# Hybrid decoder layer on one core: right-hand tiles moved by 32 bytes, value compression by broadcast behind the first value matmuls, decay series moved

## The chip, the cores and the metric

One core of one Trainium2 chip runs the whole layer in one launch. The metric is the device time of one execution in microseconds, taken over several runs; the median is compared. Engines are named as in the profile: PE is the matrix engine (PEld its weight loads), DVE the vector engine, ACT the activation engine, POOL the general engine, SP the engine that issues most DMAs.

## What is computed

The layer takes `x` of 512 tokens by 1024 and returns the same shape. All is float32.

```
h = rms_norm(x, norm1_g); proj = h @ w_in          # split into rx, rgate, q, kc, vc, ks, vs, kw, vw, gates
y_rnn = (rg_lru(causal_dwconv(rx)) * gelu(rgate)) @ w_rnn_out
   # rg_lru: log_a = 8 * r * log_sigmoid(lru_lambda); h_t = a_t h_{t-1} + u_t
v_cmp = gelu(blocks(vc) @ cmp_w1_v) @ cmp_w2_v     # 31 compressed positions, 4 groups, 64 wide; k_cmp alike, then normed
o = gates * (softmax(q k_cmp) v_cmp, softmax(q k_slc) v_slc, softmax(q k_win) v_win)    # 16 heads, 4 groups
x = x + (sigmoid(mg_rnn) * y_rnn + sigmoid(mg_attn) * (o @ w_attn_out)) @ w_out
x = x + (gelu(gate) * val) @ w_down                # gate, val = causal_dwconv(rms_norm(x) @ w_up)
```

## The kernel before

Activations stand with channels on the 128 partitions and the 512 tokens along the row. Each weight arrives as a tile of 128 x 1024 from one packed array `in_w`, in the order of a plan. `_wprep` (L115 to 138) issues its DMA on SP into one of two `wraw` tiles, ACT rounds it into `whi` (L124), and DVE, or POOL during the heads, subtracts to get the low half `wlo` (L131, or L129 in pieces of 256 columns). Three buffers each of `whi` and `wlo` stand between that and PE. A product of float32 accuracy is three matmuls (`mm3`, L153 to 155): high weight by high activation, high by low, low by high. Here the activation is the moving operand (512 columns) and the weight the loaded one; in the value projections (L669 to 671, L701 to 703) it is the other way about.

The stages, by their time in the profile: the first norm with the projections for the compressed keys and values (to 43 us); `before_heads` (to 88 us), with keys of the first pair, the hidden layers of the two compressors (`compress_hid`), two query projections, `compress_out` and `v_pair0`; sixteen heads with the other projections filled in between (to 383 us); the output projection of attention, `attn_out`, which reads `oh` and `ol` (383 to 428 us); the recurrent part (to 565 us); `merge`, whose matmuls read `hgh` and `hgl` (565 to 628 us); `w_out`, which reads `mh` and `ml` (to 671 us); the feed-forward part, whose last stage reads `fh` and `fl`.

PE's order is the order of the code (`manual_schedule`). On the other engines a scheduler sets the order of the instructions from its own estimate; `high_priority` moves one ahead in it, and `issue_after` keeps one behind a named instruction. `later` and `tick` hold small PE steps back by a number of yields of the running generator.

Tiles come from pools at either end of the memory. Pools with `side="right"` grow down from its upper end: `ea1`, `ea2` (L256, L258), `otp` with `ot`, `otl` with `oh` and `ol`, and `hgp` with `hgh`, `hgl`, `iv` and `g`. In the built program these start 32 bytes past a multiple of 64 (`oh` at 180192, `ol` at 196576, `hgh` at 186336). The tiles of the left side, with `xh`, `xl`, `mh`, `ml`, `fh`, `fl` (this one from 155840 to 204992) and the three buffers of each weight half, start at multiples of 64.

`compress_hid("v")` ends with the gelu `hidv` (L517) and then makes the four copies of it that fill 128 columns: four casts on ACT into `hv` (L524) and four subtractions on DVE into `hvl` (L525). `compress_out` (L528 on) multiplies these, as loaded weights, by the second layer (L537 to 539), then the keys' `hk` by theirs (L153 to 155 with 128 columns). After it `v_pair0` (L661 on) runs eight steps `k` with twelve matmuls of 304 columns each, from three weight tiles of three steps.

`lru_c8` (L890 on) works out `8 * log_sigmoid(lru_lambda)` by a series of 25 DVE instructions on 128 x 11 values (L896 to 907). It is called in `attn_out` after the fourth of eight output columns (L871); its result is first read in the recurrent part. The scheduler put the 25 into DVE's order in the first head.

Of the kernel before, what the change touches and what calls it, by code (L numbers as in the profile page):

```python
# [8 lines left out]
F32 = mybir.dt.float32  # L9
# [38 lines left out]
MS_L, KL1, KL2, QN_L = 3, 12, 14, 6  # L48

MS1, RT1, SQ_W = 2, 7, 4  # L50
HPRI = 200

EARLY = "mmSSSmmSSmSm"

RNN_STEPS = ("rx0 rx1 rx2 rx3 rg0 rx4 rx5 rg1 scan0 rgate0 rgate1 rg2 rgate2 rgate3 rx6 gelu0 rx7 rgate4 rgate5 rg3 "
             "scan1 rx8 rx9 rgate6 rx10 rgate7 gelu1 rgate8 rg4 rg5 scan2 rgate9 gelu2")
# [46 lines left out]
class Kern:  # L103
# [123 lines left out]
    def build(self):  # L227
        tc, nc, a = self.tc, self.nc, self.a
        tp = lambda name, **kw: tc.tile_pool(name=name, bufs=1, reuse_waits="tile", **kw)
        L = ExitStack()  # L230
        with L:
            self.cst = L.enter_context(tp("cst"))
            self.wp = L.enter_context(tp("wp"))
            xp = L.enter_context(tp("xp"))
            drp = L.enter_context(tc.tile_pool(name="drp", bufs=1, space=bass.MemoryType.DRAM))
            self.mg = {}
            for n in ("mga", "mgr"):
                for c in range(8):
                    self.mg[n, c] = drp.tile([128, S], F32, name=f"{n}{c}")
            self.pp = self.cst.tile([128, NP_], F32, name="pp")  # L240
            self.cc = self.cst.tile([128, NC_], F32, name="cc")
            self.ones = self.cst.tile([128, 128], F32R, name="ones")
            self.rstd = self.cst.tile([128, S], F32, name="rstd")
            self.rstdt = self.cst.tile([128, 4], F32, name="rstdt")
            nc.scalar.dma_start(self.pp, a["pp"])
            self.ident = self.cc[:, C_ID:C_ID + 128]
            self.xh = xp.tile([128, KO, S], F32R, name="xh")
            self.xl = xp.tile([128, KO, S], F32R, name="xl")

            R2 = ExitStack()  # L250
            with R2:
                with tp("at") as self.at, ExitStack() as at_ps, tc.manual_schedule(engines={mybir.EngineType.PE}):
                    self.ps = at_ps.enter_context(tp("psA", space=PSUM))
                    self.mmb = 2
                    self.early = 0
                    with tp("ea1", side="right") as self.ea:  # L256
                        pss = self.norm1()
                    with tp("ea2", side="right") as self.ea:  # L258
                        self.before_heads(pss)
                    self.early = None  # L260
                    otp = R2.enter_context(tp("otp", side="right"))
                    self.ot = otp.tile([128, KO, S], F32, name="ot")
                    self.mgo = at_ps.enter_context(tp("mgo"))
                    self.pool_lo = True
                    with tp("hd") as self.hd:
                        fills = self.heads()
                    otl = R2.enter_context(tp("otl", side="right"))
                    self.out_split(otl)
                    for _ in fills:
                        self.tick()  # L270
                    self.pool_lo = False
                mgp = L.enter_context(tp("mgp"))
                self.ma = mgp.tile([128, KO, S], F32, name="ma")
                PB = ExitStack()
                self.ps = PB.enter_context(tp("psB", space=PSUM))
                self.mmb = 7
                self.attn_out()
            with tp("hgp", side="right") as self.hgp:
                self.hgh, self.hgl = {}, {}
                self.wpri = 80  # L280
                with tp("rnn") as self.rn:
                    self.rnn()
                self.wpri = 0
                with tp("mrg") as self.mr:
                    self.mh = self.mr.tile([128, KO, S], F32R, name="mh")
                    self.ml = self.mr.tile([128, KO, S], F32R, name="ml")
                    self.merge()
                    self.xn = mgp.tile([128, KO, S], F32, name="xn", tag="ma")
                    self.w_out()
            with tp("ff") as self.ff:  # L290
                self.ffn()
            PB.close()
# [11 lines left out]
    def norm1(self):  # L304
# [50 lines left out]
        def token_rstd():  # L355
# [6 lines left out]
            w = at.tile([128, 4], F32, name="rsw")  # L362
            with self.tc.high_priority(HPRI):
                nc.vector.tensor_scalar(m, ms[:, :, 0], 1.0 / D, EPS, op0=ALU.mult, op1=ALU.add)
# [4 lines left out]
        def row_rstd():  # L369

            pt = self.ps.tile([128, S], F32, name="T", bufs=2)
            for t in range(4):
                nc.tensor.transpose(pt[:, 128 * t:128 * t + 128], e[:, t], self.ident)
            with self.tc.high_priority(HPRI):
                nc.scalar.copy(self.rstd, pt)
# [7 lines left out]
    def before_heads(self, pss):  # L383
        nc, at = self.nc, self.at

        self.gkq = self.cst.tile([128, 3], F32, name="gkq")
        nc.vector.tensor_scalar(self.gkq, self.pp[:, P_KS:P_KS + 3], self.pp[:, P_QG:P_QG + 1], None, op0=ALU.mult)

        self.G = at.tile([128, 4, 48], F32, name="G")
        self.kfull, self.kraw, self.qs, self.rq, self.V, self.qms = {}, {}, {}, {}, {}, {}  # L390

        self.compress_in("k", pss[:2])
        self.compress_in("v", pss[2:])
        self.run(self.k_pair(0))
        self.pool_lo = True
        self.run(self.compress_hid("k"))
        self.run(self.q_proj(0))
        self.later(1, lambda: self.k_fin(0))
        self.later(1, lambda: self.k_fin(1))
        self.run(self.compress_hid("v"))  # L400
        self.run(self.q_proj(1))
        self.later(4, lambda: self.q_norm(0))
        self.run(self.compress_out())
        self.run(self.v_pair0())

    def later(self, n, f):

# [87 lines left out]
    def compress_hid(self, kind):  # L495
        nc, at = self.nc, self.ea
        ch = getattr(self, "ch" + kind)
        ps = self.mmps()[:, 0:272].rearrange("p (s g i) -> p s g i", s=2, g=4)
        for m in range(16):
            if m % 8 == 0:  # L500
                wh, wl = self.w("w1" + kind, m // 8)
            col = slice(128 * (m % 8), 128 * (m % 8) + 128)
            q = m // 8
            nc.tensor.matmul(ps.rearrange("p s g i -> p (s g) i"), wh[:, col],
                             ch[:, :, :, m % 8, q:q + 34].rearrange("p s g i -> p (s g) i"),
                             start=(m == 0), stop=False)
            nc.tensor.matmul(ps[:, 0], wl[:, col], ch[:, 0, :, m % 8, q:q + 34],
                             start=False, stop=(m == 15))
            if m % 3 == 2:
                yield  # L510
        t = at.tile([128, 4, 34], F32, name="ct", bufs=2)
        nc.scalar.copy(t, ps[:, 1])
        nc.vector.tensor_add(t, t, ps[:, 0])
        b = at.tile([128, 1], F32, name="cb", bufs=2)
        nc.vector.tensor_copy(b, t[:, 0, 32:33])
        hid = at.tile([128, 4, 32], F32, name="hid" + kind)
        nc.scalar.activation(hid, t[:, :, 0:32], AF.Gelu_apprx_tanh, bias=b)  # L517
        if kind == "k":
            self.hk = at.tile([128, 2, 128], F32R, name="hk")
            self.split(self.hk[:, 0], self.hk[:, 1], hid.rearrange("p g i -> p (g i)"))  # L520
        else:
            self.hv = [at.tile([128, 4, 4, 32], F32R, name=n) for n in ("hv", "hvl")]
            for r in range(4):
                nc.scalar.copy(self.hv[0][:, :, r], hid)  # L524
                nc.vector.tensor_sub(self.hv[1][:, :, r], hid, self.hv[0][:, :, r].bitcast(F32))  # L525

    def compress_out(self):
        nc, at, keep = self.nc, self.ea, self.at  # L528
# [222 lines left out]
    def cmp_probs(self, g):  # L751
# [7 lines left out]
        pl = self.hd.tile([128, S], F32R, name="cpl", bufs=1)  # L759
        with self.tc.high_priority(HPRI):  # L760
            self.split(ph, pl, T)
# [96 lines left out]
    def attn_out(self):  # L858
        nc, oh, ol = self.nc, self.oh, self.ol
        self.last_tab = self.last_exp  # L860
        for k in range(KO):
            nc.sync.dma_start(self.ma[:, k], self.mg["mga", k])
            self.tab(self.ma[:, k], self.ma[:, k], AF.Sigmoid)
        for m in range(8):
            wt = self.w("ao", m)
            ps = self.ps.tile([128, S], F32, name="mm", bufs=self.mmb)
            for k in range(KO):
                self.mm3(ps, wt, slice(128 * k, 128 * k + 128), (oh[:, k], ol[:, k]), k == 0, k == KO - 1)
            nc.vector.tensor_mul(self.ma[:, m], ps, self.ma[:, m])
            if m == 3:  # L870
                self.c8 = self.lru_c8()  # L871

    def tab(self, *args, **kw):

# [365 lines left out]
```

## Time and profile before

| | |
|---|---|
| median of 3 runs | 1068.7 us (1066.21 to 1070.89) |
| the profiled execution | 1069.39 us, span of its instructions 1067.6 us |
| PE busy, of the span | 98% (1048.5 us) |
| DVE, ACT, POOL busy | 67%, 53%, 18% |
| DMA queues, memory rate | 96 GB/s mean |
| PE's waits | 1.84 us and 1.29 us between 67 and 70.5 us, 1.93 us at 115 us |

The rows further on come from this one execution. Starts are microseconds from the start of the span. A matmul's duration in a row is longer than its share of PE's time, since the next one begins before it ends: PE's pace is read from the starts. PEclk is the clock granted to PE as a share of 2.4 GHz.

### The profile page before, as it was taken

Reading aid. Unit: us, or ns where it says so; the run is one execution under the profiler, and the core shown is the slowest. Engines: PE = TensorE matmul, PEld = TensorE weight load, DVE = VectorE, ACT = ScalarE, POOL = GpSimd, SP = SyncE. Lnnn points to the kernel's source line nnn. Section 1 sums busy time; section 2 is a strip of 40 time slices with the busy share of each in tenths; the row PEclk is TensorE's granted clock in tenths of the full one; section 3 lists DMA queues with packets and bytes.
Section 4 is the critical chain, followed back from the end, with each engine's and each line's share of the span. In section 5 each row is a group of like instructions: output and inputs, shape, how many; then the busy total and the mean of one; then the engine's idle time right before and its main releaser. Section 6 shows DMA issues by size and latency. Waiting matters only on the chain.

```text
span 1067.6 us, 13868 instructions
## 1 busy us (share of the span) xinstructions
PE 1048.5 (98%) x5023; PEld 875.7 (82%) x5023; DVE 714.2 (67%) x1359; ACT 565.2 (53%) x953; POOL 192.6 (18%) x324
## 2 busy tenths in 40 slices
PE   9989999999999999999999999999999999999998
PEld 7888788978888888887877888888888888888886
DVE  6767879877777643789698564777777777732221
ACT  6366677878767641477667433444444444421110
POOL 0356325135252210231312003100000000000000
PEclk9999899999999999999999999999999999999999
DMA  6421211011221262443333534232223332333330
GB/s 242 96 98 60 59 60 40 21 70 50 67 73 67 94 195 92 116 145 103 119 100 107 197 109 148 89 109 92 97 91 95 99 99 99 99 109 119 109 112 26
DMA packets 44452, 106.04 MB, mean 99 GB/s; under 512 B 13231, under 2 KB 14639, under 8 KB 44384
## 3 DMA queue, kind: packets, MB, share of 16 engines
q1 hardware_dynamic: 41632, 102.26, 29.7%
q0 software_dynamic: 2608, 2.76, 1.1%
q8 instruction: 39, 0.64, 0.2%
q14 instruction: 29, 0.24, 0.1%
q10 hardware_dynamic: 144, 0.15, 0.0%
HBM read 96.10 MB, written 6.29 MB: 96 GB/s over the span
## 4 chain that ended last, share of the span: by engine, by line
PE 76%; DVE 11%; ACT 8%; issue 2%; DMA 2%; POOL 1%; SPq 0%; DVEq 0%; ACTq 0%
PE mm L153 22%; PE mm L155 22%; PE mm L154 22%; PE O L815 3%; ACT s L797 2%; PE T L824 2%; DMA wraw<-in_w 2%; ACT whi L124 1%; PE S L786 1%; DVE wlo L131 1%; PE S L787 1%; DVE s L790 1%; DVE ptl L179 1%; DVE iv L977 1%; ACT pth L178 1%
## 5 line engine op out<-in xcount | busy, mean ns | idle before, releaser
L124 ACT CAST whi<-wraw 128x1024 fp32r<-128x1024 f32 (+2 forms) x167 | 172.6, 1034 | 231.9 <-PE mm L154 199.5
L153 PE MATMUL mm<-xh,whi 128*128 128x512 f32 x744 | 292.6, 393 | 0.5 <-ACT hgh L178 0.5
L155 PE MATMUL mm<-xh,wlo 128*128 128x512 f32 x744 | 291.4, 392 | 1.0 <-DVE wlo L131 1.0
L154 PE MATMUL mm<-xl,whi 128*128 128x512 f32 x744 | 291.0, 391 | 0.0
L131 DVE TENSOR_TENSOR wlo<-wraw,whi 128x1024 fp32r<-128x1024 f32 (+1 forms) x131 | 158.5, 1210 | 93.2 <-ACT whi L124 91.9
L155 PEld LDWEIGHTS mm<-xh,wlo 128*128 128x128 f32 x744 | 140.2, 188 | 31.3 <-DVE wlo L131 1.4
L153 PEld LDWEIGHTS mm<-xh,whi 128*128 128x128 f32 x744 | 140.3, 189 | 29.2 <-ACT hgh L178 0.9
L154 PEld LDWEIGHTS mm<-xl,whi 128*128 128x128 f32 x744 | 140.3, 189 | 28.5
L129 POOL TENSOR_TENSOR wlo<-wraw,whi 128x256 fp32r<-128x256 f32 (+1 forms) x140 | 101.5, 756 | 221.9 <-ACT whi L124 188.3
L797 ACT ACTIVATE s<-s,bs,rq 128x128 f32<-128x128 f32 (+3 forms) x128 | 82.5, 648 | 19.4 <-DVE bs L794 19.3
L153 PE MATMUL mm<-fh,whi 128*128 128x512 f32 x192 | 74.7, 389 | 0.0
L154 PE MATMUL mm<-fl,whi 128*128 128x512 f32 x192 | 74.7, 389 | 0.0
L155 PE MATMUL mm<-fh,wlo 128*128 128x512 f32 x192 | 74.7, 389 | 0.0
L1080 DVE SCALAR_TENSOR_TENSOR y<-u,pp,y 128x512 f32<-128x512 f32 x96 | 71.7, 749 | 2.0 <-ACT y L1078 0.4
L179 DVE TENSOR_TENSOR ptl<-T,pth 128x512 fp32r<-128x512 f32 x80 | 55.0, 687 | 21.1 <-ACT pth L178 20.7
L790 DVE CUSTOM_DVE_ANT_0 s<-S,cc 128x128 f32<-128x128 f32 (+3 forms) x128 | 58.0, 483 | 6.9 <-PE S L787 6.5
L178 ACT CAST pth<-T 128x512 fp32r<-128x512 f32 x80 | 46.5, 581 | 28.4 <-PE T L824 27.9
L1076 DVE TENSOR_TENSOR u<-mm,rstd 128x512 f32<-128x512 f32 x48 | 33.0, 688 | 40.8 <-PE mm L155 40.8
L824 PE MATMUL T<-cc,s 128*128 128x128 f32 x320 | 48.8, 274 | 1.3 <-DVE ptl L179 0.8
L824 PEld LDWEIGHTS T<-cc,s 128*128 128x128 f32 x320 | 39.5, 141 | 12.5 <-DVE ptl L179 1.3
L1075 POOL MEMSET u<- 128x2 f32 x48 | 4.7, 100 | 246.0 <-DVE y L1080 241.7
L178 ACT CAST fh<-y 128x512 fp32r<-128x512 f32 x24 | 14.9, 621 | 63.7 <-DVE y L1087 63.7
(299 smaller groups left out, 1870.1 us busy)
## 6 DMA issues: line engine op xcount, KB each, us to landing
wraw<-in_w SPq DMA_DIRECT2D x158, 512.0 KB, 3.4
x<-in_x SPq DMA_DIRECT2D x8, 256.0 KB, 4.5
mga<-mgo SPq DMA_DIRECT2D x8, 256.0 KB, 2.0
mgr<-mgo SPq DMA_DIRECT2D x8, 256.0 KB, 2.5
ma<-mga SPq DMA_DIRECT2D x8, 256.0 KB, 4.3
sg<-mgr SPq DMA_DIRECT2D x8, 256.0 KB, 3.6
xr<-in_x SPq DMA_DIRECT2D x8, 256.0 KB, 2.7
out<-y SPq DMA_DIRECT2D x8, 256.0 KB, 2.0
```

The source lines that it names most:

```text
L124: self.last_hi = nc.scalar.copy(hi[:, :n], raw[:, :n])
L129: nc.gpsimd.tensor_sub(lo[:, e], raw[:, e], hi[:, e].bitcast(F32))
L131: nc.vector.tensor_sub(lo[:, :n], raw[:, :n], hi[:, :n].bitcast(F32))
L153: nc.tensor.matmul(ps, wh, xh, start=first, stop=False)
L154: nc.tensor.matmul(ps, wh, xl, start=False, stop=False)
L155: nc.tensor.matmul(ps, wl, xh, start=False, stop=last)
L178: self.nc.scalar.copy(hi, src)
L179: self.nc.vector.tensor_sub(lo, src, hi.bitcast(F32))
L790: nc.vector.tensor_tensor_reduce(s[i, x], ps[:, x - xs[0]], mask, 1.0, -3e38, ALU.add, ALU.max, mx[:, x, i:i + 1])
L797: self.last_exp = nc.scalar.activation(s[t, x], s[t, x], AF.Exp, bias=bs[:, x, t:t + 1], scale=rq[:, t], accum_out=sm[:, x, t:t + 1])
L824: nc.tensor.transpose(T[:, off:off + 128], s[i, x][:, 128 * j:128 * j + 128], self.ident)
L1080: nc.vector.scalar_tensor_tensor(y, u[:, j:j + S], pc(P_FW, j * nu + c), y, ALU.mult, ALU.add)
```

## The change

The right-hand side gets a first tile of 32 bytes, so that every right-hand tile moves down by 32 bytes (`oh` to 180160, `ol` to 196544, `hgh` to 186304) and starts at a multiple of 64. The four casts and four subtractions for `hv` and `hvl` become one of each, reading `hidv` by broadcast, and get the priority. The first four yields of `v_pair0` (two of its eight steps, 24 matmuls) run before `compress_out`; for that the accumulator of the values' second layer moves from the tag `S` to `mm`. The 25 instructions of the decay series are kept behind the fourth `ma` product.

```diff
-EARLY = "mmSSSmmSSmSm"
+EARLY = "mmSSSmmSSmmm"
+VP0 = 4
...
+            L.enter_context(tp("rpad", side="right")).tile([128, 8], F32, name="rpad")
...
+        v = self.v_pair0()
+        for _ in range(VP0):
+            next(v)
+            self.tick()
         self.run(self.compress_out())
-        self.run(self.v_pair0())
+        self.run(v)
...
-            for r in range(4):
-                nc.scalar.copy(self.hv[0][:, :, r], hid)
-                nc.vector.tensor_sub(self.hv[1][:, :, r], hid, self.hv[0][:, :, r].bitcast(F32))
+            h4 = hid.rearrange("p g (o i) -> p g o i", o=1).to_broadcast([128, 4, 4, 32])
+            with self.tc.high_priority(HPRI):
+                nc.scalar.copy(self.hv[0], h4)
+                nc.vector.tensor_sub(self.hv[1], h4, self.hv[0].bitcast(F32))
...
-            nc.vector.tensor_mul(self.ma[:, m], ps, self.ma[:, m])
+            ins = nc.vector.tensor_mul(self.ma[:, m], ps, self.ma[:, m]).ins
             if m == 3:
-                self.c8 = self.lru_c8()
+                with self.tc.issue_after(ins):
+                    self.c8 = self.lru_c8()
```

The new lines shift the numbers: a line of the changed program stands up to ten lower (L537 becomes L546, L669 becomes L678).

PE, at the end of the second query projection, before (`em` the accumulator, `hv` and `hvl` the value copies):

```order
L155 MATMUL em<-xh,wlo 128x512
L537 MATMUL em<-whi,hv 128x64
L538 MATMUL em<-wlo,hv 128x64
L539 MATMUL em<-whi,hvl 128x64
L537 MATMUL em<-whi,hv 128x64
```

and the same place in the changed program (`v_724` to `v_727` are the accumulators of `v_pair0` for its four blocks of 128 tokens):

```order
L156 MATMUL em<-xh,wlo 128x512
L678 MATMUL v_724<-whi,xh 128x304
L679 MATMUL v_724<-wlo,xh 128x304
L680 MATMUL v_724<-whi,xl 128x304
L678 MATMUL v_725<-whi,xh 128x304
...
L679 MATMUL v_727<-wlo,xh 128x304
L680 MATMUL v_727<-whi,xl 128x304
L546 MATMUL em<-whi,hv 128x64
```

The matmuls on `hv` stood right behind the projection; 24 value matmuls, with four small `hsq` matmuls among them, now stand between.

DVE in the first head, before, between the score maxima of head 1 (`ISA s,mx`) and the copy of `qms` that frees an accumulator `T`; rows with `lt`, `ly` and `ls` are the series:

```order
L896 TENSOR_SCALAR lt<-ly 128x11
L794 SCALAR_TENSOR_TENSOR bs<-mx,rq 128x4
L897 RECIPROCAL lt<-lt 128x11
L898 TENSOR_TENSOR ls<-ly,lt 128x11
L899 TENSOR_TENSOR lt<-ls 128x11
L900 TENSOR_SCALAR ly<-lt 128x11
L902 TENSOR_TENSOR ly<-ly,lt 128x11
L179 TENSOR_TENSOR ptl<-T,pth 128x512
...
L179 TENSOR_TENSOR ptl<-T,pth 128x512
L575 COPY qms<-T 128x4x2
```

and in the changed program from the same `bs` on:

```order
L803 SCALAR_TENSOR_TENSOR bs<-mx,rq 128x4
L180 TENSOR_TENSOR ptl<-T,pth 128x512
L799 ISA s_1228,mx<-S,cc 128x384
L799 ISA mx 128x1
L799 ISA s_1233,mx<-S,cc 128x512
L799 ISA mx 128x1
L803 SCALAR_TENSOR_TENSOR bs<-mx,rq 128x4
L808 RECIPROCAL sm<-sm 128x4
L809 TENSOR_TENSOR sm<-sm,G 128x4
L811 TENSOR_SCALAR s_1145<-s_1145,sm 128x128
L180 TENSOR_TENSOR ptl<-T,pth 128x512
L584 COPY qms<-T 128x4x2
```

Sixteen instructions of the series stood ahead of the copy in this piece and the nine others followed within five microseconds; now none stands there.

DVE in `attn_out` in the changed program (`ma` the products, `wlo` the weights' low halves):

```order
L878 TENSOR_TENSOR ma<-mm,ma 128x512
L906 TENSOR_SCALAR lt<-ly 128x11
L132 TENSOR_TENSOR wlo<-wraw,whi 128x1024
L907 RECIPROCAL lt<-lt 128x11
L908 TENSOR_TENSOR ls<-ly,lt 128x11
...
L914 TENSOR_TENSOR ly<-ly,ls 128x11
L878 TENSOR_TENSOR ma<-mm,ma 128x512
L916 TENSOR_TENSOR lt<-lt,ly 128x11
L132 TENSOR_TENSOR wlo<-wraw,whi 128x1024
L917 TENSOR_SCALAR c_4584<-lt 128x11
```

Before, `ma` and `wlo` alone took turns there; now 22 instructions of the series stand between one `wlo` and the next `ma`, one ahead of that `wlo` and two behind that `ma`.

## Rows read from the trace of the kernel before

**Rows 1.** The page: busy time of PE; granted PE clock in 40 slices, in tenths.

```profile
PE 1048.5 (98%) x5023; PEld 875.7 (82%) x5023; DVE 714.2 (67%) x1359; ACT 565.2 (53%) x953; POOL 192.6 (18%) x324
PEclk9999899999999999999999999999999999999999
```

**Rows 2.** Instructions by tile: min/median/max ns, first to last start.

```profile
L153 PE MATMUL mm<-oh,whi x64: 393/396/399, 383.4 to 427.5; 128*128 128x512 f32 x64
L153 PE MATMUL mm<-hgh,whi x88: 389/396/403, 565.6 to 627.0; 126*128 126x512 f32 x80, 84*128 84x512 f32 x8
L153 PE MATMUL mm<-mh,whi x64: 389/389/397, 627.7 to 670.6; 128*128 128x512 f32 x64
L153 PE MATMUL mm<-fh,whi x192: 389/389/389, 932.9 to 1062.8; 128*128 128x512 f32 x192
```

**Rows 3.** Timeline of PE, 66 to 83 us: start, us, [idle before <-releaser].

```profile
66.61 0.39 PE L155 MATMUL em<-xh,wlo 128*128 128x512 f32 x1
68.84 0.30 PE L537 MATMUL em<-whi,hv 128*128 128x64 f32 x1 [1.84 <-ACT hv L524]
70.53 0.30 PE L539 MATMUL em<-whi,hvl 128*128 128x64 f32 x1 [1.29 <-DVE hvl L525]
...
82.27 0.30 PE L669 MATMUL v<-whi,xh 128*128 128x304 f32 x1
82.69 0.30 PE L669 MATMUL v<-whi,xh 128*128 128x304 f32 x1
```

**Rows 4.** Windows: us, busy (x) of PE, PEld, DVE, ACT, POOL; PEclk, DMA.

```profile
72.20:75.60 3.40, 3.40 (x17) 3.40 (x15) 1.12 (x2) 1.78 (x5) 2.28 (x5) 0.50 0.53 165
116.60:123.40 6.80, 6.24 (x21) 5.39 (x22) 5.26 (x31) 3.96 (x8) 0.00 (x0) 0.50 0.01 2
383.40:428.00 44.60, 44.60 (x193) 35.81 (x192) 15.44 (x17) 8.39 (x8) 0.00 (x0) 1.00 0.35 113
```

**Rows 5.** Timeline of ACT, DVE and POOL, 66 to 73 us.

```profile
66.60 0.95 ACT L124 CAST whi<-wraw 128x912 fp32r<-128x912 f32 x1 [1.34 <-DMA wraw<-in_w]
67.89 0.90 ACT L524 CAST hv<-hidv 128x128 fp32r<-128x128 f32 x4
...
68.22 2.26 DVE L525 TENSOR_TENSOR hvl<-hidv,hv 128x128 fp32r<-128x128 f32 x4 [0.80 <-ACT hv L524]
...
67.63 5.27 POOL L129 TENSOR_TENSOR wlo<-wraw,whi 128x256 fp32r<-128x256 f32 x8 [2.62 <-ACT whi L124]
```

**Rows 6.** Timeline of PE, 114 to 124 us.

```profile
117.16 1.09 PE L757 MATMUL T<-cc,cl 128*128 128x128 f32 x4 [1.93 <-DVE qms L575]
...
119.54 0.63 PE L154 MATMUL mm<-xl,whi 128*128 128x512 f32 x1
```

**Rows 7.** Timeline of DVE, 108 to 125 us.

```profile
109.83 0.70 DVE L898 TENSOR_TENSOR ls<-ly,lt 128x11 f32<-128x11 f32 x1
...
114.40 0.17 DVE L902 TENSOR_TENSOR ly<-ly,lt 128x11 f32<-128x11 f32 x1
114.61 0.17 DVE L903 TENSOR_SCALAR ly<-ly 128x11 f32<-128x11 f32 x1
...
116.33 0.68 DVE L179 TENSOR_TENSOR ptl<-T,pth 128x512 fp32r<-128x512 f32 x1
116.93 0.15 DVE L575 COPY qms<-T 128x8 f32<-128x8 f32 x1
...
124.28 0.29 DVE L790 CUSTOM_DVE_ANT_0 s<-S,cc 128x128 f32<-128x128 f32 x1 [1.98 <-PE S L787]
```

**Rows 8.** Timeline of ACT, 112 to 125 us.

```profile
113.10 0.57 ACT L178 CAST pth<-T 128x512 fp32r<-128x512 f32 x1
...
124.03 0.59 ACT L178 CAST pth<-T 128x512 fp32r<-128x512 f32 x1 [1.72 <-PE T L824]
```

**Rows 9.** Timeline of DVE, 400 to 420 us.

```profile
406.02 0.69 DVE L869 TENSOR_TENSOR ma<-mm,ma 128x512 f32<-128x512 f32 x1 [3.53 <-PE mm L155]
406.86 1.23 DVE L131 TENSOR_TENSOR wlo<-wraw,whi 128x1024 fp32r<-128x1024 f32 x1 [0.15 <-ACT whi L124]
```

## The prediction

> **What bounds it now.** Read the page of the profile first: PE is busy 1048.5 of 1067.6 us, and its clock is full in nearly every slice [rows 1]. So an engine other than PE only matters where PE waits for it, and two things can shorten the run: a shorter PE instruction, or a stretch in which PE stands still or runs at the lower clock. Then read three views. The instructions by tile [rows 2] give PE's pace stage by stage: in each group of three matmuls one is on L153, so first and last start, divided by the matmuls between, is the interval. The timeline of PE [rows 3, 6] shows the two places with the waits that this change aims at. The windows [rows 4] show what clock was granted right behind them. I add up against the profiled execution, 1069.39 us, which is 0.7 us over the median of 1068.7.
>
> **Part 1, the 32 bytes.** In `attn_out` 63 groups of three lie between 383.4 and 427.5 us: 44.1 / 189 = 0.2333 us a matmul. `w_out` does the same kind and number in 42.9 / 189 = 0.2270, and the last stage takes 129.9 / 573 = 0.2267 [rows 2]. `merge`, over 261 intervals, takes 61.4 / 261 = 0.2352, a short wait included. All have 512 columns, and `attn_out` has them at the full clock [rows 4]. The two slow stages are those whose moving operand lies on the right side at 32 past a multiple of 64; the two quick ones read tiles at multiples of 64. 126 partitions in place of 128 do not explain it, since `oh` has 128; nor does a high address, since `fl` reaches past 200000. I take the difference to `w_out`, 0.0064 us, for 192 matmuls of `attn_out` and 264 of `merge`: 456 x 0.0064 = **2.9 us**, all on PE's path. The bounds are 0, if the place is not the cause, and 3.8, if all of `merge`'s figure is pace (192 x 0.0064 + 264 x 0.0082 = 3.4) and the compressor's 64 matmuls, whose moving tiles lie on the right side too, gain as much each (0.4).
>
> The Trainium skill has a rule that speaks against this part. Its page SBUF — State Buffer, in the sections Specifications (TRN2) and SBUF: two separate sides, counts lines of 16 bytes and lets PE wait for nobody on its own ports; a start of 32 past 64 lies on such a line, so by that page nothing is gained and the sum would be 2.9 us smaller. The two paces above are what the rule leaves unexplained, so I go by the rows.
>
> **Part 2, compression by broadcast behind 24 value matmuls.** Before, the projection's last matmul starts at 66.61; the first on `hv` waits 1.84 us for ACT's copies, the first on `hvl` 1.29 us for DVE's subtractions [rows 3]. These are the last in a line: ACT casts a weight (66.60, held by its DMA), then the gelu, four copies (0.90 us), and DVE's four subtractions end at 70.48 [rows 5]. In the changed order PE first meets the 24 value matmuls. Their high weight is that very cast, done at 67.55; their low weight comes from POOL from 67.63 on, eight pieces in 5.27 us, so 0.66 each [rows 5]. The second matmul reads columns of two pieces: about 69.0. PE is then idle from 67.0 to 69.0 but for one matmul of 0.14: about 2.0 us in place of 3.13, **1.1 us** less. After that 24 matmuls at 0.42 / 3 = 0.14 [rows 3] last 3.3 us, to 72.3, before anything needs `hvl`. The single cast is unseen: between 0.53 (512 of 912 columns of the cast of 0.95) and the present 0.90. The single subtraction lies between 0.68 (a 128x512 one in rows 7) and the present 2.26. Even the dear ends give 71.1, so 24 matmuls cover them and I count them as nothing; without that cover they would cost what they cost now. Bounds of the wait: 0.6 us if only the cast counts, 3.1 if the low weight comes as late as `hvl` did; a gain of 0 to 2.5. What is late next is that low weight from POOL. The change of tag makes the keys' second layer wait for DVE's last `qs` subtraction, which stands behind the `hsq` matmuls that go among the 24; I put it at 0, at most 0.7.
>
> Then the clock: from 72.20 to 75.60 it is 0.50, 1.2 of 2.4 GHz [rows 4], right behind that wait and behind twelve matmuls of only 64 columns. PE was busy all of it, so half was lost: **1.7 us**, which I take as won, because full-size matmuls now fill 69 to 72.
>
> **Part 3, the series.** PE waits 1.93 us before the transposes at 117.16, for the copy of `qms` on DVE, which frees an accumulator [rows 6]. That copy stands at 116.93 behind a `ptl` at 116.33 [rows 7], and ahead of both stood sixteen instructions of the series: some at 0.70, some at 0.17 with 0.21 from start to start. Five of the long ones and eleven of the short ones are about 5 us of DVE's time. Without them the `ptl` can follow its cast on ACT, which began at 113.10 and took 0.57 [rows 8], and end with its own 0.68 at 114.4, the copy behind it at 114.5: before PE gets there at 117.16 - 1.93 = 115.2. So **1.9 us**. Behind the wait the clock is 0.50 from 116.60 to 123.40, with PE busy 6.24 us [rows 4]; a matmul of 512 columns lasts 0.63 there [rows 6] against 0.39 at full clock [rows 3]. Half of 6.24 is **3.1 us**. Is it only moved? At 124.28 DVE had waited 1.98 us for PE, and at 124.03 ACT 1.72 [rows 7, 8]: both had caught up, so what PE does earlier they do earlier.
>
> Where the 25 instructions go, DVE waits 3.53 us for PE in each column and POOL does nothing [rows 9, 4]. At 0.21 each the 22 between take 4.6 us against 3.53 + 0.15 free: the next `ma` slips by a microsecond, and the low weight behind it too. That is the last column's, due at 413.7 (a column after 406.86, and 1.23 long), and PE begins that column at 383.4 + 7 x 5.6 = 422.6, nine later: 0. With every one at 0.70 they take 15.4 us, against 9 and 3.5 of slack, and PE would lose 3 us. I take the low end, for the short price is that of the great majority. Three ACT and three DVE instructions fall away: nothing, under PE.
>
> **The sum.** 2.9 + 1.1 + 1.7 + 1.9 + 3.1 = 10.7; 1069.4 - 10.7 = 1058.7, and with the median's 0.7 below the profile I say **1058.5 us**.
>
> **The rivals.** *The place of the tiles costs nothing* and something else slows the two stages, such as the work of the other engines in them. For it: DVE and ACT do work beside `merge`; against it: in `attn_out` they hardly do (15 and 8 of 45 us [rows 4]) and the pace is the same. Then 1069.4 - 7.8 = 1061.6. The Trainium skill's rule (SBUF — State Buffer, the two sections above) gives this one too.
>
> *The clock is not won back*: the falls come anyway, here or elsewhere, because PE still stands 2.0 us at 67 and starts later stages earlier against other engines. For it: a wait of that size preceded both falls. Against: each fell behind a longer spell of little work than will be left. Then only 5.9 us are won: 1063.5.
>
> *The heads take part 3 back*, since DVE and ACT are the busiest there and PE runs into the next of them. Against it are the two waits at 124 us. Then 1069.4 - 5.7 = 1063.7.
>
> *Slower: the series stalls the weights of `attn_out`.* DVE works in order, so the low weight of the last column waits behind 22 instructions. Its present slack is nine microseconds and DVE's idle 3.5: PE starts to wait when they cost over 0.56 us each, and the gain of 10.7 is gone at about 1.05. At 1.5 each PE would lose 20.6 us: 1079.3. The dearest row is 0.70 and POOL is idle there, so it is unlikely.
>
> **The numbers.** The forecast has a chance of 0.60, the first rival 0.12, the second 0.13, the third 0.07, the last 0.03; 0.05 is for two of the gains failing at once, at about 1066. A measurement of this kernel can tell 0.5%, 5.3 us, from no change: the line is 1063.4. The forecast and the first rival lie below it, the second and third on it, of which I count half: faster 0.82, same 0.15, slower 0.03. The range takes in the forecast with its bounds (0.9 more from part 1, 1.4 more from the wait at 67 us, and the rest of a microsecond for the spread of runs) and the first three rivals: 1055.5 to 1064.0.
>
> **What would show it.** By tile, first and last start of the `oh` matmuls 42.9 us apart and those of `hgh` 60 us. In PE's timeline, value matmuls from 67.6, a wait for POOL's `wlo` to 69, none for `hv` or `hvl`; no wait before the transposes of `cl`. The granted clock full behind both places. DVE's series after the fourth `ma`, at 0.17 each, and no wait of PE on `wlo` in `attn_out`. Part 1 is wrong if the `oh` pace stays at 0.233; part 2 if PE waits past 70; part 3 if the wait at 115 has only another name; the sum is wrong if a clock of 0.50 shows up behind a place that had none.

## The result, and the profile after

The changed kernel takes 1061.27 us (median of 5 runs, 1059.81 to 1062.85) against 1070.7 for the kernel before (5 runs, 1066.21 to 1071.31). By the means of these runs the ratio is 0.992, with a 95% interval of 0.9897 to 0.9944: faster by 8.5 us, 6 to 11 (the medians lie 9.4 apart). The profiled execution, the quickest of the five, takes 1059.81 us with a span of 1058.0; forecast for it were 1058.7.

The page answers to [rows 1]; busy time of the engines, and the granted clock in 40 slices:

```profile
PE 1041.6 (98%) x5023; PEld 871.8 (82%) x5023; DVE 716.3 (68%) x1357; ACT 564.3 (53%) x949; POOL 193.2 (18%) x324
...
PEclk9999999999999999999999999999999999999999
```

PE is still the bound; 6.9 us of its busy time and 2.7 us of its idle time are gone. Where they went is read from the first and last starts of tiles that both kernels have. Instructions by tile of the changed kernel, duration ns min/median/max, then first and last start; `kcs` are the narrow score matmuls of heads 0, 4, 8 and 12, the others answer to [rows 2]:

```profile
L729 PE MATMUL S<-kcs,qs x64: 193/277/278, 92.6 to 294.9; 128*128 128x64 f32 x64
L154 PE MATMUL mm<-oh,whi x64: 389/389/389, 376.1 to 418.9; 128*128 128x512 f32 x64
L154 PE MATMUL mm<-hgh,whi x88: 387/389/503, 557.0 to 617.5; 126*128 126x512 f32 x80, 84*128 84x512 f32 x8
L154 PE MATMUL mm<-mh,whi x64: 389/389/393, 618.2 to 661.0; 128*128 128x512 f32 x64
L154 PE MATMUL mm<-fh,whi x192: 389/389/389, 923.3 to 1053.2; 128*128 128x512 f32 x192
```

and the same first row of the kernel before:

```profile
L720 PE MATMUL S<-kcs,qs x64: 193/277/277, 94.9 to 302.2; 128*128 128x64 f32 x64
```

The lead over the kernel before is 2.3 us at the first `kcs` (94.9 - 92.6), 7.3 at the last (302.2 - 294.9) and still 7.3 where `oh` begins (383.4 - 376.1), 8.6 at its end, 8.6 where `hgh` begins, 9.5 at its end, and 9.6 at the last `fh` (1062.8 - 1053.2). So each part shows as one step of this stair, and nothing is taken back between the steps. `w_out`, whose tiles did not move, keeps its pace: 42.8 us for `mh`, 42.9 before [rows 2].

Step one, by the timeline of PE (start, us, idle before and its releaser), answers to [rows 3]:

```profile
67.03 0.39 PE L156 MATMUL em<-xh,wlo 128*128 128x512 f32 x1
68.22 0.41 PE L678 MATMUL v<-whi,xh 128*128 128x304 f32 x1 [0.80 <-ACT whi L125]
69.71 0.41 PE L679 MATMUL v<-wlo,xh 128*128 128x304 f32 x1 [1.09 <-POOL wlo L130]
...
73.89 0.19 PE L546 MATMUL em<-whi,hv 128*128 128x64 f32 x1
```

The two waits are now 0.80 for ACT's cast and 1.09 for POOL's low half; 24 value matmuls follow and the ones on `hv` find their operand ready. ACT, DVE and POOL there, answering to [rows 5]:

```profile
68.24 5.53 POOL L130 TENSOR_TENSOR wlo<-wraw,whi 128x256 fp32r<-128x256 f32 x8 [2.79 <-ACT whi L125]
68.50 0.62 ACT L533 CAST hv<-hidv 128x512 fp32r<-128x512 f32 x1
69.15 1.05 DVE L534 TENSOR_TENSOR hvl<-hidv,hv 128x512 fp32r<-128x512 f32 x1 [1.27 <-ACT hv L533]
```

`hvl` is there at 70.2, 3.7 us before the first matmul on `hv`. The windows (us, busy and count of PE, PEld, DVE, ACT, POOL; PEclk, DMA) answer to [rows 4]:

```profile
72.20:75.60 3.40, 3.40 (x31) 3.40 (x31) 2.19 (x8) 0.52 (x2) 1.57 (x3) 1.00 0.51 151
108.00:124.00 16.00, 16.00 (x94) 13.80 (x93) 14.33 (x51) 12.46 (x30) 5.10 (x8) 1.00 0.22 68
228.80:232.20 3.40, 2.95 (x7) 2.40 (x8) 3.00 (x13) 2.12 (x6) 1.75 (x4) 0.50 0.00 0
```

In this execution the clock is full at 72 us and from 108 to 124, where PE doesn't stop at all; a fall at 229 us, which the kernel before had at 236, is still there. The series on DVE answers to [rows 7, 9]:

```profile
398.06 0.69 DVE L878 TENSOR_TENSOR ma<-mm,ma 128x512 f32<-128x512 f32 x1 [3.36 <-PE mm L156]
...
398.93 1.23 DVE L132 TENSOR_TENSOR wlo<-wraw,whi 128x1024 fp32r<-128x1024 f32 x1
400.07 0.22 DVE L907 RECIPROCAL lt<-lt 128x11 f32<-128x11 f32 x1
...
404.31 0.68 DVE L878 TENSOR_TENSOR ma<-mm,ma 128x512 f32<-128x512 f32 x1
```

Twenty-two instructions take from 400.07 to 404.31, 4.2 us; the `ma` behind them is 0.8 us later than one column's time after the last (24 matmuls at 0.2265, 5.44 us), and PE loses nothing.

### The profile page after: what moved, and what is told of

It is laid out like the page before. It is cut to its first block, busy times and chain, and to the rows that moved or that the text cites. A ratio compares the mean times of both kernels' runs of the same rounds, so it can differ in the third digit from the quotient of the medians.

```text
span 1058.0 us, 13861 instructions
## 1 busy us (share of the span) xinstructions
PE 1041.6 (98%) x5023; PEld 871.8 (82%) x5023; DVE 716.3 (68%) x1357; ACT 564.3 (53%) x949; POOL 193.2 (18%) x324
## 4 chain that ended last, share of the span: by engine, by line
PE 77%; DVE 9%; ACT 8%; DMA 3%; issue 2%; POOL 1%; SPq 0%; DVEq 0%; ACTq 0%; POOLq 0%
PE mm L154 22%; PE mm L155 22%; PE mm L156 22%; PE O L824 3%; PE T L833 2%; ACT s L806 2%; DMA wraw<-in_w 2%; PE S L795 1%; ACT whi L125 1%; PE S L796 1%; DVE wlo L132 1%; DVE iv L987 1%; ACT pth L179 1%; DVE s L799 1%; ACT r L886 1%
```

## The experiments

Eleven other kernels ran, and the changed one once more. The last columns give the mean time and the mean granted clock over the runs of each, and the runs of the kernel before that were made beside them. Where a step is small it is read from the traces, since a run's time moves by several microseconds for another cause (below).

| run | runs | median us | ratio to before (95%) | mean us, clock | before beside it |
|---|---|---|---|---|---|
| right32_alone | 12 | 1067.42 | 0.9988 (0.9971 to 1.0005) | 1067.7, 0.9912 | 1069.2, 0.9922 |
| right64_alone | 12 | 1068.37 | 0.9992 (0.9975 to 1.001) | 1068.5, 0.9933 | the same |
| values_alone | 12 | 1066.30 | 0.997 (0.9956 to 0.9984) | 1066.0, 0.9944 | the same |
| series_alone | 12 | 1065.06 | 0.997 (0.9952 to 0.9988) | 1065.8, 0.9932 | the same |
| broadcast_alone | 12 | 1068.61 | 0.9993 (0.998 to 1.0007) | 1068.3, 0.9928 | 1068.9, 0.9930 |
| early24_alone | 12 | 1066.06 | 0.997 (0.9955 to 0.9985) | 1065.6, 0.9946 | the same |
| left32_moved | 4 | 1076.61 | 1.0071 (1.0044 to 1.0099) | 1076.4, 0.9955 | the same |
| weights32_moved | 4 | 1078.61 | 1.009 (1.0066 to 1.0114) | 1078.7, 0.9960 | the same |
| all32_moved | 6 | 1060.14 | 0.9918 (0.9891 to 0.9946) | 1060.1, 0.9957 | 1068.9, 0.9928 |
| changed_again | 6 | 1059.81 | 0.9915 (0.9888 to 0.9941) | 1059.8, 0.9963 | the same |
| lows_last | 6 | 1060.78 | 0.9926 (0.9899 to 0.9953) | 1061.0, 0.9978 | the same |
| head7_only | 6 | 1059.35 | 0.9906 (0.988 to 0.9931) | 1059.2, 0.9973 | 1069.3, 0.9924 |

### Each part alone

**right32_alone** is the kernel before with one line of the change, the one that makes the `rpad` tile.

> The kernel before with the 32-byte tile on the right side and nothing else; the order on every engine stays as it was. Theory (the start of a moving tile past a multiple of 64 bytes sets PE's pace): first and last start of the oh matmuls 42.9 us apart in place of 44.1, the hgh ones about 60.5 in place of 61.4, the whole 2.2 to 2.9 us shorter than before, and the two waits at 67 to 70 us and the one at 115 us stay. Rival (the place costs nothing, the gain in those two stages came with the other parts): 44.1 and 61.4 us as before, no gain.

Instructions by tile:

```profile
L153 PE MATMUL mm<-oh,whi x64: 389/389/389, 386.5 to 429.3; 128*128 128x512 f32 x64
L153 PE MATMUL mm<-hgh,whi x88: 389/389/502, 567.4 to 627.8; 126*128 126x512 f32 x80, 84*128 84x512 f32 x8
```

42.8 and 60.4 us in place of 44.1 and 61.4 [rows 2], with no instruction moved: 2.3 us, and the first rival is out. The mean is 1.5 us lower and the interval of the ratio takes in 1, because 2.3 us is less than these runs can tell; the trace tells it.

**right64_alone** is the control, the same line with 16 in place of 8, so that the tiles move down by 64 bytes and are again 32 past a multiple.

> Control of the first: the right-hand tile is 64 bytes in place of 32, so every right-hand tile moves down by 64 and still starts at 32 past a multiple of 64. Theory (the start past a multiple of 64 counts): the oh matmuls 44.1 us apart as before, no gain. Rival (any move down, or another neighbour in memory, is what helps): 42.9 us as with 32 bytes.

```profile
L153 PE MATMUL mm<-oh,whi x64: 395/396/397, 383.0 to 427.1; 128*128 128x512 f32 x64
```

44.1 us, as before: moving the tiles is not enough.

**values_alone** is the kernel before with the lines of the change for the 24 matmuls, the tag and the broadcast.

> The kernel before with 24 value matmuls ahead of the second layer, the broadcast and the accumulator's tag, and nothing else. Theory: waits of about 0.8 us (cast of the weight on ACT) and 1.1 us (low weight on POOL) in place of 1.84 and 1.29, none for hv or hvl, no fall of the clock at 72 us, 2.3 to 2.8 us ahead behind 78 us; the wait and the fall at 115 us stay as before. Rival (the clock falls anyway): 1.1 us ahead.

Timeline of PE:

```profile
67.74 0.39 PE L155 MATMUL em<-xh,wlo 128*128 128x512 f32 x1
68.94 0.41 PE L674 MATMUL v<-whi,xh 128*128 128x304 f32 x1 [0.81 <-ACT whi L124]
70.42 0.41 PE L675 MATMUL v<-wlo,xh 128*128 128x304 f32 x1 [1.08 <-POOL wlo L129]
```

The waits are those of the whole change. By tile, `kcs` begins at 93.3, against 94.9 before, and PE came to this place 1.1 us later (67.74 against 66.61): 2.7 us won. The waits make 1.2 of it (1.89 us in place of 3.13); the rest goes with the fall of the clock at 72 us, which this execution does not have. The mean is 3.2 us below the kernel before.

**series_alone** is the kernel before with the last lines of the change, those that keep the series behind the fourth `ma`.

> The kernel before with the 25 instructions of the series kept behind the fourth ma and nothing else. Theory: PE's wait of 1.93 us before the transposes at 115 us is gone, the clock stays full from 116.6 to 123.4 us, and PE is 5.0 us ahead behind 125 us and stays so to the end; no wait of PE on wlo in attn_out. Rival A (the heads take it back): the lead shrinks to under 2 us before 380 us. Rival B (the clock falls all the same): a lead of 1.9 us.

`kcs` by tile, and the window from 108 to 124 us with one of an earlier stretch:

```profile
L720 PE MATMUL S<-kcs,qs x64: 193/277/278, 93.6 to 296.0; 128*128 128x64 f32 x64
```

```profile
108.00:124.00 16.00, 16.00 (x93) 13.78 (x92) 14.22 (x49) 12.95 (x30) 5.95 (x9) 1.00 0.21 67
59.40:66.20 6.80, 6.80 (x26) 6.12 (x26) 6.52 (x10) 5.72 (x11) 4.74 (x6) 0.50 0.27 83
```

No wait at 115 us and a full clock; the lead grows from 1.3 (94.9 - 93.6) to 6.2 (302.2 - 296.0): 4.9 us, and it stays. The mean is 3.4 us lower, less than 4.9. The second window shows why a single trace says too much: here the clock fell at 59 us, where the profile of before had it full.

### The falls of the clock are not tied to a place

right64_alone puts every instruction in the order of the kernel before, and its waits at 72 and 118 us are there, the one for `hv` shorter (0.48 in place of 1.84), since PE came to it 3.8 us later. PE's timeline, and the windows:

```profile
71.31 0.30 PE L538 MATMUL em<-whi,hv 128*128 128x64 f32 x1 [0.48 <-ACT hv L525]
73.01 0.30 PE L540 MATMUL em<-whi,hvl 128*128 128x64 f32 x1 [1.28 <-DVE hvl L526]
...
118.07 0.63 PE L758 MATMUL T<-cc,cl 128*128 128x128 f32 x4 [1.95 <-DVE qms L576]
```

```profile
62.20:65.60 3.40, 3.40 (x17) 3.21 (x16) 3.24 (x6) 3.29 (x6) 3.40 (x4) 0.53 0.09 29
70.00:76.00 6.00, 4.23 (x30) 3.66 (x29) 3.37 (x6) 3.82 (x11) 5.26 (x8) 1.00 0.22 79
116.60:123.40 6.80, 5.33 (x34) 4.81 (x35) 6.71 (x40) 5.23 (x11) 0.00 (x0) 1.00 0.01 2
185.20:188.60 3.40, 3.40 (x11) 2.81 (x12) 2.82 (x8) 2.81 (x9) 0.00 (x0) 0.52 0.02 5
```

Behind both waits the clock is full, where it was 0.50 in [rows 4]; the falls came at 62 and 185 us instead. So which of its weak stretches an execution pays for changes from one to the next. The 35 runs of the kernel before that were made beside these four show it as a whole: the 11 with a mean clock of 0.990 took 1070.87 to 1072.26 us, the 10 with 0.993 took 1065.98 to 1069.27, the 5 with 0.995 took 1065.79 to 1067.18, the one with 0.996 took 1065.30. Most of the spread of this kernel goes with the clock. What a removed wait is worth in clock is its share in all executions, so it is read from the mean clock: 0.0022 higher with the values alone (0.9944 against 0.9922), which is 2.3 us of 1068; 0.0010 with the series alone, 1.1 us. The second is not clear of noise: right64_alone's mean is 0.0011 higher with no order changed.

The fourteen profiled executions side by side say more. The table gives the mean granted clock of three stretches, by where the part of the change that bears on them stands.

| stretch, us | with the old place | with the new place |
|---|---|---|
| 69 to 80 (values) | before 0.84, right32_alone 0.69, three others 1.00 | nine executions, all 1.00 |
| 108 to 130 (series) | before and right32_alone 0.84, values_alone and early24_alone 0.92, right64_alone and broadcast_alone 1.00 | eight executions, all 1.00 |
| 180 to 192 (series) | values_alone, early24_alone, right64_alone and broadcast_alone 0.86, before and right32_alone 1.00 | eight executions, all 1.00 |

With the series in the first head each of the six executions has a fall in one of the last two stretches or in both, which costs 1.7 to 3.5 us (an estimate: the missing share of the clock times the length); with the series in `attn_out` none has one. So the clock is won back, though a fall is not tied to one place. How much of it belongs to which part stays open: by these executions about 1 us to the values and 3 to the series, by the mean clocks about 2 and 1.

### Which half of part 2 matters

**early24_alone** keeps the four casts and four subtractions, **broadcast_alone** keeps PE's order; their edits are the two halves of that of values_alone, the tag with the first.

> The kernel before with the 24 value matmuls ahead of the second layer and the accumulator's tag, and the four casts and four subtractions kept. Theory (24 matmuls, 3.3 us, cover even the dear form): the same waits as with all of part 2, 0.8 and 1.1 us, none for hv or hvl, the same gain within 0.3 us. Rival (the broadcast or its priority is needed): a wait for hvl of 0.5 us or more behind the 24.

> The kernel before with the four casts and four subtractions made one of each by broadcast, with priority, and PE's order as before. Theory (the 24 value matmuls are the cover; the broadcast only shortens the line): the first wait, 1.84 us for hv, is shorter by 0 to 0.4, the second, 1.29 for hvl, by about 1.2 to 1.5 (one subtraction of about 0.7 in place of 2.26), PE 1.2 to 1.9 us ahead behind 72 us. Rival (broadcast reads are dear, 2 us each): no gain.

early24_alone, PE's timeline from 68 to 76 us, has one wait:

```profile
70.81 0.41 PE L674 MATMUL v<-wlo,xh 128*128 128x304 f32 x1 [0.62 <-POOL wlo L129]
```

and none for `hv` or `hvl`. (In this execution the clock fell at 62 us, PE came at 69.7 in place of 66.6, and the cast was ready.) DVE's four subtractions end at 72.2 here and PE asks for their result at 75.1. Its mean is 3.3 us below the kernel before, that of both halves together 3.2. broadcast_alone's is 0.6 below, inside the error; the 1.2 to 1.9 us expected of it did not come. Its timeline of PE:

```profile
69.59 0.30 PE L538 MATMUL em<-whi,hv 128*128 128x64 f32 x1
...
70.69 0.30 PE L540 MATMUL em<-whi,hvl 128*128 128x64 f32 x1 [0.69 <-DVE hvl L526]
...
76.43 0.49 PE L556 MATMUL T<-kc,cc 128*128 128x128 f32 x2 [0.65 <-ACT kc L551]
```

PE came later in this execution and found `hv` ready. The wait for `hvl` is 0.6 us shorter than the 1.29 before, and 0.65 comes back at 76 us in a wait for ACT that the trace of before does not have. From the projection's last matmul to the first `kcs` it takes 25.34 us (69.06 to 94.40), and right64_alone, with the four copies, 25.35 (70.44 to 95.79), both at the full clock. So the 24 matmuls are the cover, as the prediction had it, and the broadcast adds nothing that can be measured.

### Why the 32 bytes count

Two kernels put tiles that were at multiples of 64 off them. **left32_moved** takes the left side from `xh` on, **weights32_moved** the weights alone:

```diff
+            xp.tile([128, 8], F32, name="xpad")
```

```diff
+            self.wp.tile([128, 8], F32, name="wpad")
...
+            xp.tile([128, 8], F32, name="xpad")
```

> The changed kernel with 32 bytes put ahead of xh on the left side, so that xh, xl, mh, ml, fh, fl and the attention's tiles start at 32 past a multiple of 64, the weights and the right side at multiples. Theory (start of the moving tile): w_out and the last stage at 0.2333 us a matmul (first to last start of the fh matmuls about 133.7 us in place of 129.9, of mh 44.1 in place of 42.9), oh and hgh stay at 0.2270; some 2350 matmuls of 512 columns on the left by 0.0064 = 15 us, with the attention's 15 to 18 us slower than the changed kernel. Rival (only the right side shows it): no difference.

> The changed kernel with 32 bytes put ahead of the weights' tiles and 32 behind them, so that only wraw, whi and wlo start at 32 past a multiple of 64. Theory (only the moving operand's start counts; the load of a weight lies beside the matmul before it): stages that load the weights stay at 0.2270; only the value projections, which move them, slow down, 192 matmuls by 0.003 to 0.004, 0.7 us in all. Rival (any read of PE counts): 0.2333 everywhere, 18 us slower.

left32_moved by tile:

```profile
L154 PE MATMUL mm<-oh,whi x64: 389/389/402, 376.9 to 419.8; 128*128 128x512 f32 x64
L154 PE MATMUL mm<-fh,whi x192: 393/395/397, 934.9 to 1068.6; 128*128 128x512 f32 x192
```

weights32_moved by tile:

```profile
L154 PE MATMUL mm<-oh,whi x64: 392/396/397, 377.2 to 421.3; 128*128 128x512 f32 x64
L154 PE MATMUL mm<-fh,whi x192: 393/396/397, 937.6 to 1071.3; 128*128 128x512 f32 x192
```

The first came out as expected: `fh` 133.7 us in place of 129.9, `oh` unchanged, the mean some 16 us above the changed kernel's. The second did not: with every moving tile where the changed kernel has it, both stages pace at 0.2333 (44.1 / 189, 133.7 / 573), and the run is 18 us slower than the changed kernel. The load of a weight does not hide its place. In all slow cases so far the two operands of a matmul start at different places within 64 bytes; equal and both off had not been tried. **all32_moved** does that:

```diff
-            L.enter_context(tp("rpad", side="right")).tile([128, 8], F32, name="rpad")
+            L.enter_context(tp("lpad")).tile([128, 8], F32, name="rpad")
```

> The changed kernel with the 32 bytes put ahead of everything on the left side in place of the right, so that weights, moving tiles of both sides and constants all start at 32 past a multiple of 64. The runs with only the moving tiles or only the weights at 32 both paced at 0.2333 us. Theory A (PE slows when either operand is off a multiple of 64): 0.2333 in every stage, oh 44.1 us from first to last start, fh 133.7, some 17 us slower than the changed kernel. Theory B (PE slows when the two operands start at different places within 64 bytes): 0.2270 everywhere, oh 42.9, fh 129.9, the time of the changed kernel. Theory C (each operand off adds its own share): above 0.2333 where both are off.

```profile
L154 PE MATMUL mm<-oh,whi x64: 389/389/389, 375.7 to 418.6; 128*128 128x512 f32 x64
L154 PE MATMUL mm<-fh,whi x192: 389/389/389, 922.9 to 1052.8; 128*128 128x512 f32 x192
```

Full pace in both, and the time of the changed kernel (1060.14 against 1059.81). Theory B stands: what counts is that weight and moving operand start at the same place within 64 bytes, not that either is at a multiple. Why, no run here shows; other distances than 32 were not tried.

### Two attempts to go further

**changed_again** is the changed kernel once more, beside all32_moved and lows_last.

> The changed kernel itself, for more of its runs. Theory (two things set the time of a run: PE's own length, shorter by 2.3 to 2.5 us through the places and 2 to 3 through the waits, and how often the clock falls in that run): runs spread over 3 to 5 us, long where the mean granted clock is low; mean 7.5 to 9 us under the kernel before; the mean clock 0.994 to 0.996 against 0.992 to 0.993. Rival (the falls are gone for good): every run within 1 us at 0.997.

Six runs lie between 1058.99 and 1060.60 us, 9.0 below the mean of before, at a clock of 0.9963. The spread is 1.6 us, less than expected.

**lows_last** moves two things on PE:

```diff
                 nc.tensor.matmul(pss[t], self.xh[:, k, tok], wh[:, col], start=(k == 0), stop=False)
-                nc.tensor.matmul(pss[t], self.xh[:, k, tok], wl[:, col], start=False, stop=False)
-                nc.tensor.matmul(pss[t], self.xl[:, k, tok], wh[:, col], start=False, stop=(k == KO - 1))
+                nc.tensor.matmul(pss[t], self.xl[:, k, tok], wh[:, col], start=False, stop=False)
+                if k:
+                    nc.tensor.matmul(pss[t], self.xh[:, k, tok], wl[:, col], start=False, stop=(k == KO - 1))
...
+            if k == 0:
+                for t in range(4):
+                    tok = slice(128 * t, 128 * t + 128)
+                    nc.tensor.matmul(pss[t], self.xh[:, k, tok], wl[:, col], start=False, stop=False)
...
                     self.cmp_scores(h // 4 + 1)
+                    fill(FILL_RATE)
+                    for _ in range(ns):
+                        next(nx, None)
+                    continue
```

> The changed kernel with two more moves on PE: in the first value step the eight matmuls on high weights ahead of the four on the low one, and in heads 3, 7 and 11 the projection steps that followed the two score steps behind the compressed scores put ahead of them. Theory: the wait of 1.09 us for POOL shrinks by 0.9 to 1.0; the waits of 1.12, 1.77 and 0.39 us behind the compressed scores shrink by up to 1.3 each, 2.8 in all, and the fall at 229 us goes with them (1.5): 3 to 5 us shorter than the changed kernel. Rival (DVE and ACT bound those heads, the wait only moves behind the projection steps): 1 us from the values alone.

The waits in its timeline of PE:

```profile
69.61 0.82 PE L691 MATMUL v<-wlo,xh 128*128 128x304 f32 x4
...
175.48 0.63 PE L844 MATMUL T<-cc,s 128*128 128x128 f32 x4 [1.06 <-DVE ptl L180]
...
230.71 0.47 PE L806 MATMUL S<-kh,qs 128*128 128x512 f32 x1 [0.39 <-DVE cs L745]
...
243.14 0.33 PE L844 MATMUL T<-cc,s 128*128 128x128 f32 x1 [0.90 <-ACT s L822]
...
308.45 0.66 PE L844 MATMUL T<-cc,s 128*128 128x128 f32 x4 [1.58 <-DVE ptl L180]
```

and in head 7 of the changed kernel:

```profile
229.25 0.77 PE L795 MATMUL S<-kh,qs 128*128 128x512 f32 x1 [1.77 <-DVE cs L734]
```

The view shows no wait for POOL any more, but only 0.15 us of the 0.9 expected there is won (25.38 us from the projection's last matmul to the first `kcs`, against 25.53 in changed_again). The wait of 1.77 at 229 us is down to 0.39. But others stand behind, longer than in the changed kernel: 1.00 at 170 and 1.06 at 175 (0.27 and 0.16 there) and 1.58 at 308 (0.44) for DVE, 0.90 at 243 for ACT (none). In heads 3 and 11 the rival holds, those engines are the bound and the wait only moves. The mean is 1.2 us above changed_again's although its clock is the highest (0.9978 against 0.9963).

**head7_only** keeps the move in head 7 alone, and nothing in the values.

```diff
                     self.cmp_scores(h // 4 + 1)
+                    if h == 7:
+                        fill(FILL_RATE)
+                        for _ in range(ns):
+                            next(nx, None)
+                        continue
```

> The changed kernel with the one of the moves of the run before that won by itself: in head 7 the two projection steps behind the score steps put ahead of them, behind the compressed scores. There it won 2.95 us (the wait of 1.76 us down to 0.39, no fall behind it) and gave 1.86 back at 243 us in a wait for ACT. Theory: 1.1 us ahead of the changed kernel behind 245 us and to the end, 0.9 to 1.3; mean clock 0.997. Rival (the fall at 229 us comes in few executions, so that on the mean only 0.3 is won or less): the changed kernel's mean within 0.5 us.

By tile, `kcs`, of it and of changed_again:

```profile
L734 PE MATMUL S<-kcs,qs x64: 193/277/278, 93.2 to 294.6; 128*128 128x64 f32 x64
```

```profile
L729 PE MATMUL S<-kcs,qs x64: 193/277/278, 92.4 to 294.8; 128*128 128x64 f32 x64
```

0.8 us behind at the first, 0.2 ahead at the last: 1.0 us won, as expected. Its six runs lie between 1058.53 and 1059.46 us, median 1059.35, the lowest of the study. Against changed_again that is 0.5 us, and the two were not run side by side: in the runs the gain is not shown.

## Why the prediction was right

**The sum.** Forecast were 10.7 us of the profiled execution, and it is 9.6 shorter. By step of the stair: the values 2.7 in place of 2.8 (2.3 of lead, and PE came 0.4 later, 67.03 against 66.61, for something ahead of the change); the series 5.0 as forecast; `attn_out` 1.3 in place of 1.2; `merge` 0.9 in place of 1.7. The median came out 2.8 above the forecast in the first five runs and 1.3 above in the six of changed_again, inside the range both times. Of the 2.8, 1.1 is what the sum gave too much. Most of the rest is in which execution was profiled: the one of after, at a clock of 0.997, is 1.5 below the median of its five (the other four have 0.994 or 0.995), while the one of before was 0.7 above the median of its three. That the sum came within 1.1 us of a single execution is in part luck. (The forecast's last step has a slip as well: 0.7 below 1058.7 is 1058.0, not 1058.5.)

**Part 1.** The price was right, 0.0064 us a matmul, and `merge` was the term that was sized too high: at 576 us PE waits for a low half that DVE makes. PE's timeline after:

```profile
575.93 0.50 PE L155 MATMUL mm<-hgl,whi 84*128 84x512 f32 x1 [0.58 <-DVE hgl L180]
```

and before:

```profile
584.55 0.51 PE L154 MATMUL mm<-hgl,whi 84*128 84x512 f32 x1 [0.34 <-DVE hgl L179]
```

The lead there is 8.6 us (584.55 - 575.93), the same as where `hgh` begins: what PE won in the first 19 us of the stage it gave back in this wait. That is about 0.5 of the 0.8 us missing; the rest is not traced. The stated cause, a moving operand off a multiple of 64, was too narrow: it was the place against the weight's (all32_moved). The rival that the place costs nothing is out: with 32 bytes alone the pace of `oh` went from 0.2333 to 0.2265 us. The prediction had drawn that rival from the lines of 16 bytes that the Trainium skill's page SBUF — State Buffer (Specifications (TRN2)) counts; here the measurement differs from what was drawn.

**Part 2.** Waits of 0.80 and 1.09 us against 2.0 with a matmul between; the low half came at 69.7, forecast 69.0, because the cast started 0.6 later (67.21 against 66.60). The single cast took 0.62 and the single subtraction 1.05, inside the bounds, and neither mattered: the 24 matmuls cover the dear form too (early24_alone).

**Part 3.** DVE's copy no longer holds the transposes and PE doesn't stop. The copy comes right behind its `ptl`, as forecast: 112.15 and the 2.3 us of lead make 114.45, forecast 114.5. Timeline of DVE after:

```profile
112.15 0.17 DVE L584 COPY qms<-T 128x8 f32<-128x8 f32 x1
```

The rival that the heads take it back is out: the lead is 7.3 us at the last `kcs` and at the first `oh`. The series costs nothing where it went: 0.19 us each (4.24 / 22), taken as 0.21. The slower rival had its threshold at 0.56 and was far. The low price was taken because most rows have it; the trace of before shows a better reason. Of the five long rows that the prediction counts, one is not of the series (`bs`, L794). The other four, 0.65 to 0.70 us, started from 109.83 to 111.95, beside this work of POOL:

```profile
106.80 5.77 POOL L129 TENSOR_TENSOR wlo<-wraw,whi 128x256 fp32r<-128x256 f32 x8 [0.31 <-ACT whi L124]
```

Two short ones lie beside it too, but the ten behind it all took 0.16 or 0.17 us, and so did nearly all in `attn_out`, where POOL does nothing. No run tests this by itself.

**The clock.** This is the other step that was mis-sized. It took 1.7 and 3.1 us from one execution's falls as if every execution had them there. In the profile of after they are gone, so against that one execution the sum held; but over the runs the mean clock rose by 0.0035 (changed_again's 0.9963 against 0.9928 of before beside it), 3.7 us rather than 4.8, and which execution is profiled decides a few microseconds by itself. The rival that the clock is not won back is out too, by these means and by the table of fourteen executions; what it says of falls that come elsewhere is true of the kernel before.

## What to carry to other kernels

Compare the paces of stages that issue the same matmul: a difference of 3% showed a tile placed 32 bytes off its partner, and 18 us hung on it for the whole kernel when the weights were moved. When a wait goes, price the clock behind it from the mean clock of many runs and from several profiled executions, not from one, and set a control with the same order beside them: here its mean clock differed by 0.0011 with nothing changed in the order. And find the step that does the covering before making anything cheaper: here PE's order did all of it. A move that won in one head lost in two others, so try such moves one at a time.

## What was not expected of the hardware

A matmul of 128x512 took 0.2270 us from start to start when the loaded and the moving operand began at the same place within 64 bytes, both at 0 or both at 32, and 0.2333 when one was at 0 and the other at 32, whichever it was. And the clock did not fall at the same places in two executions of the same order: full behind the wait of 1.95 us before the transposes in right64_alone, 0.50 behind the same wait of 1.93 in the profile of before.
